# Sampled attention stream: the order of key gathers and value gathers on GpSimd

## Chip, cores, metric

The kernel runs on one core of a Trainium2 chip as a single launch. The metric is the device time of that launch in microseconds (us). The engines are named as in the profile: PE is TensorE (PEld its weight loads), DVE VectorE, ACT ScalarE, POOL GpSimd, SP SyncE (it only issues transfers).

## What is computed

One inference step of a one-layer decoder. A prompt of 2048 tokens and 8 sampled sequences of 8 new tokens each go through a shared input projection, then through FoX attention (softmax attention with a forgetting bias) beside an mLSTM, an output projection, layer norm, a squared-ReLU MLP and a second layer norm. The part that the change touches is the attention of the sampled tokens over a paged cache of 8192 old keys and values for each sequence:

```python
k_past = cache_k[l][page_table].reshape(DB, past, FOX_HEADS, FOX_HEAD_DIM)
v_past = cache_v[l][page_table].reshape(DB, past, FOX_HEADS, FOX_HEAD_DIM)
...
s_past = jnp.einsum('bqhd,bkhd->bhqk', q, k_past).astype(jnp.float32) * scale
s_past = s_past + Ln[..., :, None] + R[:, :, None, :]
...
p = jax.nn.softmax(jnp.concatenate([s_past, s_new], axis=-1), axis=-1).astype(v_new.dtype)
o = jnp.einsum('bhqk,bkhd->bqhd', p[..., :P], v_past) + jnp.einsum('bhqk,bkhd->bqhd', p[..., P:], v_new)
```

Keys and values together are 512 pieces of 512 KB (256 of each, 128 partitions by 1024 float32), fetched page by page through the page table.

## The kernel before

The prompt's work is done in stages: the input projection with the mLSTM (stage B and M in the code's letters, up to about 920 us), the prompt's FoX attention (about 920 to 1340 us), the output projection (about 1340 to 1600 us) and the MLP (about 1600 us to the end, matmuls into `ph` and `py`). The sampled attention is a Python generator, `sample_attention`, whose 295 steps are traced in between that work: `tick` counts the prompt's matmul time, and each time a pace is exceeded one more `step(n)` of the generator is traced. No step is traced during the prompt's FoX attention.

Within a step the names are:

- `k_gather(n)` (L1665) issues one indirect transfer from POOL that lands one key piece in the ring `kT`. Four pieces make a group. `k_turn(n)` (L1670) transposes a landed piece in place on DVE. `qk_step(g)` multiplies the queries with group g on PE into `sQ` (L1697) and thereby frees the ring's places.
- `v_gather()` (L1774) issues two indirect transfers from POOL (L1785), the two halves of one value step, into a pair of buffers. `vt` is always there; a second pair, `vx` in the output projection and `xr` in the MLP, is lent by the prompt's work. `pv_step` multiplies the softmax weights with these halves on PE into `sO` (L1809), the second half first, and thereby frees the pair.
- For the first 19 groups (`GA`), the ring holds one group: pieces 4g to 4g+3 are fetched in two steps after `qk_step(g-1)`. From group 19 on, the ring holds three pairs of pieces, and step n fetches piece n into the place of piece n-6. One `qk_step(k-1)` then frees the places of four pieces: 4k+2 and 4k+3, which complete group k, and 4k+4 and 4k+5, the first half of group k+1.

All instructions are laid out by a scheduler that replays a timeline while it orders each engine's queue; a program's order on PE, DVE, ACT and POOL is what it finds, within the dependencies and the priorities of the traced order. `tc.issue_after(ins)` is a hint to it alone: instructions traced within the block stand behind `ins` on that engine's queue, and no semaphore is added. Each engine then works through its queue in order, so on POOL a gather that waits for a place holds up everything behind it, the layer norms of the prompt's work (L173, L177) and the mLSTM's products (L765, L767) included.

Of the kernel before, what the change touches and what calls it, by code (L numbers as in the profile page):

```python
# [1530 lines left out]
def sample_attention(tc, I, O, ps_, pps, cst, ident, sqk, dnl, dR, dmix, dqb, vx, kx, pe, ring_a):  # L1531

    nc = tc.nc
    V, A, G, T, SY = nc.vector, nc.scalar, nc.gpsimd, nc.tensor, nc.sync
# [32 lines left out]
    cv = I["cache_v"][0].rearrange("g (t f) h d -> (g t) (f h d)", f=2)  # L1567
# [48 lines left out]
    for g in range(2):  # L1616
        p = pps.tile([32, 8, 64], F32, name="sT", tag="sX", bufs=1)
# [22 lines left out]
    def piece(n):  # L1640

        return kx["ring"][:, n // 2 % 2, n % 2] if n < NA else kx["ring"][:, (n - NA) // 2 % 3, n % 2]

    def q_load(b):
        qt = ps_.tile([128, 2, 16, 8], F32, name="qt", bufs=2)
        for n in range(2):
            SY.dma_start(qt[:, n].rearrange("p d t -> p (d t)"), dap(dqb, (n * NB + b) * 4096, [[0, 4], [128, 32], [1, 128]]))
        bn = ps_.tile([128, 2, 8], F32, name="bn", bufs=2)
        for hg in range(2):
            SY.dma_start(bn[:, hg], dap(dnl, hg * 4 * TOT + S + b * 8, [[TOT, 4], [0, 32], [1, 8]]))  # L1650
        state[b] = dict(qt=qt, bn=bn, U=[])
# [11 lines left out]
        mx = ps_.tile([128, 2, 17], F32, name="mxs", bufs=2)  # L1663
        z.update(qb=qb, kr=z["qt"][:, 1], Sn=Sn, mx=mx)

    def k_gather(n):
        b, j = divmod(n, 32)
        G.indirect_dma_start(out=piece(n), out_offset=None, in_=ck, in_offset=IO(ap=idxK[:, b, j // 2, j % 2:j % 2 + 1], axis=0))  # L1668

    def k_turn(n):  # L1670

        for i in range(2):
            x = piece(n)[:, i * 512:(i + 1) * 512]
            V.transpose(x, x)  # L1674
# [8 lines left out]
    def qk_step(g):  # L1683

        b, kt = divmod(g * 2, 16)
        z = state[b]
        rb = z["rb"]
        a0 = piece(4 * g)
        d = 1 if g < GA else (2 * (g - GA) + 1) % 3 - 2 * (g - GA) % 3
        pq = pps.tile([128, 2, 256], F32, name="sQ", tag="sX", bufs=1)  # L1690
        for hg in range(2):
            for db in range(2):
                for h4 in range(4):
                    hd = (hg * 4 + h4) * 2 + db
                    kv = bass.AP(tensor=a0.tensor, offset=a0.offset + hd * 32,
                                 ap=[list(a0.ap[0]), [d * 2048, 2], [512, 4], [1, 32]])
                    r = T.matmul(pq[h4 * 32:h4 * 32 + 32, hg].rearrange("p (k f c) -> p k f c", k=2, f=4), z["qb"][:, hd], kv,  # L1697
                                 start=(db == 0), stop=(db == 1), skip_group_check=True)
        if kt % 4 == 0:
            z["U"].append(ps_.tile([128, 2, 4, 4, 32], F32, name="S", tag="S", bufs=4))  # L1700
        for k in range(2):
            c = slice(k * 128, k * 128 + 128)
            for hg in range(2):
                V.tensor_tensor_reduce(out=z["U"][kt // 4][:, hg, :, kt % 4 + k], in0=pq[:, hg, c].rearrange("p (b t) -> p b t", t=32),
                                       in1=rb[:, hg, c].rearrange("p (b t) -> p b t", t=32), scale=1.0, scalar=NEG,
                                       op0=OP.add, op1=OP.max, accum_out=z["mx"][:, hg, kt + k:kt + k + 1])
        return r

    def softmax(b):
        z = state[b]  # L1710
        pq = pps.tile([128, 2, 256], F32, name="sQ", tag="sX", bufs=1)
        for hg in range(2):
            for db in range(2):
                for h4 in range(4):
                    hd = (hg * 4 + h4) * 2 + db
                    T.matmul(pq[h4 * 32:h4 * 32 + 32, hg, 0:8], z["qb"][:, hd], z["kr"][:, hd],
                             start=(db == 0), stop=(db == 1), skip_group_check=True)
        for hg in range(2):
            V.tensor_tensor_reduce(out=z["Sn"][:, hg], in0=pq[:, hg, 0:8], in1=z["bn"][:, hg], scale=1.0, scalar=NEG,
                                   op0=OP.add, op1=OP.max, accum_out=z["mx"][:, hg, 16:17])  # L1720

        V.tensor_reduce(mt[:, 0:2], z["mx"], axis=AX.X, op=OP.max)
        m2 = ps_.tile([128, 32], F32, name="m2", bufs=2)
        V.transpose(m2, mt)
        m3 = ps_.tile([128, 8], F32, name="m3", bufs=2)
        V.tensor_reduce(m3, m2.rearrange("p (g q) -> p q g", q=8), axis=AX.X, op=OP.max, negate=True)
        V.tensor_copy(m2.rearrange("p (g q) -> p g q", q=8), m3[:, None, :].to_broadcast([128, 4, 8]))
        m4 = ps_.tile([128, 32], F32, name="m4", bufs=2)
        V.transpose(m4, m2)
        rp = z["rp"] = ps_.tile([128, 2, 5], F32, name="rp", bufs=2)  # L1730
        for u in range(4):
            for hg in range(2):
                x = z["U"][u][:, hg].rearrange("p b k t -> p (b k t)")
                A.activation(x, x, AF.Exp, bias=m4[:, hg:hg + 1], accum_out=rp[:, hg, u:u + 1])
        for hg in range(2):
            A.activation(z["Sn"][:, hg], z["Sn"][:, hg], AF.Exp, bias=m4[:, hg:hg + 1], accum_out=rp[:, hg, 4:5])
# [34 lines left out]
    def v_new(b):  # L1771
        vn = state[b]["vn"] = ps_.tile([8, 512], F32, name="vns", bufs=1)
        SY.dma_start(vn, O["v_sample"][0, b].rearrange("t h d -> t (h d)"))

    def v_gather():

        p = vx["next"]
        b, kt = divmod(p, 16)
        vx["next"] += 1
        place = 0 if 0 not in vx["live"] else 1  # L1780
        vx["live"].append(place)
        vx["of"][p] = []
        for f in range(2):
            vt = (ps_.tile([128, 1024], F32, name="vt", bufs=2) if place == 0 else vx["more"]()).rearrange("p (f c) -> p f c", f=2)
            G.indirect_dma_start(out=vt.rearrange("p f c -> p (f c)"), out_offset=None, in_=cv,  # L1785
                                 in_offset=IO(ap=idxV[:, b, (kt % 4) * 4 + kt // 4, f:f + 1], axis=0))
            vx["of"][p].append(vt)

    def v_room():
        return kx["free"] and vx["next"] < 128 and len(vx["live"]) < (2 if vx["more"] else 1) and (0 not in vx["live"] or vx["more"])  # L1790
# [43 lines left out]
    def at(n, first, of):  # L1834

        i, r = divmod(n - first, of)
        return i if r == 0 and i >= 0 else None
# [4 lines left out]
    def step(n):  # L1842
        after = None
        if n == 0:
            q_load(0)
        g, r = divmod(n - 2, 4)
        if 0 <= g < GA and r >= 2:
            k_turn(4 * g + 2 * r - 4)
            k_turn(4 * g + 2 * r - 3)
        if NA + 2 < n < 258:  # L1850
            if n == NA + 3:
                k_turn(NA)
            k_turn(n - 2)
        g = at(n, 6, 4)
        if g is not None and g < 64:
            after = qk_step(g)
        b = at(n, 35, 32)
        if b is not None and b < 8:
            softmax(b)
        due = (n - 38) // 2 if n > NA + 2 else (n - 39) // 2  # L1860
        lead = 2
        while done[0] < 128 and done[0] - (lead == 1 and done[0] % 2) <= due and got.get(done[0], n) <= n - lead:
            after = pv_step(done[0] // 16, done[0] % 16, after)
            done[0] += 1
            lead = 1
        b = at(n, 70, 32)
        if b is not None:
            pv_end(b)
        b = at(n, 39, 32)
        if b is not None and b < 8:  # L1870
            softmax_new(b)
            v_new(b)
        b = at(n, 41, 32)
        if b is not None and b < 8:
            softmax_sum(b)
        u = at(n, 37, 8)
        if u is not None and u < 32:
            for hg in range(2):
                weights(u // 4, u % 4, hg)
        b = at(n, 30, 32)  # L1880
        if b is not None and b < 7:
            q_load(b + 1)
        b = at(n, 3, 32)
        if b is not None and b < 8:
            q_begin(b)
        g = at(n, 4, 4)
        if g is not None and g < 64:
            r_load(g)
        if n >= 35 and (n % 2 == 1 or not vx["live"]):
            while v_room():  # L1890
                got[vx["next"]] = n
                v_gather()
        g, r = divmod(n - 2, 4)
        if 0 <= g < GA and r < 2:
            k_gather(4 * g + 2 * r)
            k_gather(4 * g + 2 * r + 1)
        if NA + 6 <= n < 256:
            k_gather(n)

    done, got = [0], {}  # L1900
    for n in range(295):
# [32 lines left out]
```

## Time and profile before

| | us |
|---|---|
| median of 3 runs | 3321.62 (3318.09 to 3328.27) |
| the profiled execution's own time | 3319.55 |
| its span, first to last instruction | 3317.4 |
| PE busy | 3208.5 |
| DVE busy | 2120.5 |
| ACT busy | 1356.3 |
| POOL busy | 927.7 |
| mean granted TensorE clock | 0.991 |

The busy times are unions over an engine's instructions; PE's includes matmuls that overlap in its pipeline. The idle time of PE in the span is 3317.4 - 3208.5 = 108.9 us. The queries used below are the list of waits (who was idle, until what came, the total, the number and the longest), the timeline (start, duration, engine, line, what is written and read, how many merged, and in brackets the idle time before it and what ended it) and the windows (busy time of each engine in a stretch, then the granted clock, the busy share of the 16 DMA engines and the rate).

### The profile page before, as it was taken

To read this page: it belongs to the slowest core of one execution; us is meant where nothing else is said; L and a number is where in the kernel's file an instruction comes from. 1 tells how busy PE (TensorE), PEld (TensorE's weight loads), DVE (VectorE), ACT (ScalarE), POOL (GpSimd) and SP (SyncE) were. 2 spreads that over 40 slices of the span, in tenths; PEclk is the share of its full clock that TensorE was granted. 3 is DMA by queue.
4 is the path that set the end of the run, shared out by engine and by line. 5 is a ranking of instruction groups with operands and counts; after the bars stand their busy time and mean duration, and the time that the engine had idled before them with its cause. 6 is when DMAs were issued, how large, how long until landed. Compare 5 with 4: busy or idle time off the path is not lost. (4 is left out here: it accounts for less than half of the span.)

```text
span 3317.4 us, 57296 instructions
## 1 busy us (share of the span) xinstructions
PE 3208.5 (97%) x21420; PEld 2635.4 (79%) x21420; DVE 2120.5 (64%) x5161; ACT 1356.3 (41%) x2670; POOL 927.7 (28%) x1060
## 2 busy tenths in 40 slices
PE   9999999899999999999999999999999999999998
PEld 8998797787877777677777777777767777889997
DVE  6857567567577777555666667666666545655555
ACT  4444245344367777312333333232333333433332
POOL 0111122322344444465332225324252210100001
PEclk9999999999999999999999999999999999999999
DMA  5665765877642223677776778768587654532222
GB/s 173 167 191 179 217 212 183 262 253 236 221 123 84 77 83 115 245 277 259 269 265 226 267 239 316 246 231 289 200 281 263 205 182 141 162 127 87 87 82 67
DMA packets 427293, 646.22 MB, mean 195 GB/s; under 512 B 83148, under 2 KB 320016, under 8 KB 426120
## 3 DMA queue, kind: packets, MB, share of 16 engines
q1 hardware_dynamic: 350184, 363.09, 36.3%
q0 software_dynamic: 74304, 270.57, 22.0%
q10 hardware_dynamic: 2528, 8.91, 0.7%
q8 instruction: 169, 2.77, 0.3%
q14 instruction: 108, 0.88, 0.1%
HBM read 589.63 MB, written 52.83 MB: 194 GB/s over the span
## 5 line engine op out<-in xcount | busy, mean ns | idle before, releaser
L1489 DVE TENSOR_TENSOR y<-y,py 128x512 f32<-128x512 f32 x475 | 319.6, 680 | 277.2 <-PE py L159 262.2
L149 ACT ACTIVATE wh<-wr 128x1024 fp32r<-128x1024 f32 x268 | 278.4, 1056 | 472.9 <-PE py L159 256.8
L1674 DVE STREAM_TRANSPOSE kT<-kT 128x512 f32<-128x512 f32 x512 | 329.7, 685 | 219.0 <-DMA kT<-cache_k,idxK 218.5
L1668 POOL DMA_INDIRECT kT<-cache_k,idxK x256 | 264.9, 1035 | 715.4 <-PE sQ L1697 588.9
L157 PE MATMUL ph<-x1h,wh 128*128 128x512 f32 (+1 forms) x1280 | 454.1, 355 | 3.8 <-ACT wh L149 2.8
L158 PE MATMUL ph<-x1l,wh 128*128 128x512 f32 (+1 forms) x1280 | 452.7, 354 | 1.2 <-DVE x1l L152 1.2
L159 PE MATMUL ph<-x1h,wl 128*128 128x512 f32 (+1 forms) x1280 | 450.6, 353 | 1.9 <-DVE wl L152 1.7
L157 PE MATMUL py<-wh,h 128*128 128x512 f32 x1024 | 401.4, 397 | 4.6 <-DVE y L1489 3.4
L158 PE MATMUL py<-wl,h 128*128 128x512 f32 x1024 | 401.9, 393 | 0.2 <-DVE wl L152 0.2
L159 PE MATMUL py<-wh,h 128*128 128x512 f32 x1024 | 402.0, 393 | 0.0
L152 DVE TENSOR_TENSOR wl<-wr,wh 128x1024 fp32r<-128x1024 f32 x268 | 334.1, 1254 | 83.6 <-PE ph L159 36.2
L157 PE MATMUL pm<-whi,xhT 128*128 128x256 f32 (+2 forms) x1040 | 302.7, 291 | 2.4 <-ACT acb L542 1.4
L158 PE MATMUL pm<-wlo,xhT 128*128 128x256 f32 (+2 forms) x1040 | 298.3, 287 | 0.0
L159 PE MATMUL pm<-whi,xlT 128*128 128x256 f32 (+2 forms) x1040 | 297.3, 286 | 0.0
L157 PEld LDWEIGHTS ph<-x1h,wh 128*128 128x128 f32 x1280 | 241.1, 188 | 39.1 <-ACT wh L149 3.0
L159 PEld LDWEIGHTS ph<-x1h,wl 128*128 128x128 f32 x1280 | 241.0, 188 | 37.3 <-DVE wl L152 3.5
L158 PEld LDWEIGHTS ph<-x1l,wh 128*128 128x128 f32 x1280 | 241.2, 188 | 35.6 <-issue 2.5
L1785 POOL DMA_INDIRECT vt<-cache_v,idxV x156 | 155.6, 997 | 323.8 <-PE sO L1809 267.2
L157 PEld LDWEIGHTS py<-wh,h 128*128 128x128 f32 x1024 | 192.6, 188 | 53.0 <-issue 9.0
L1451 ACT ACTIVATE hq<-ph 128x512 f32<-128x512 f32 (+1 forms) x160 | 82.6, 516 | 361.0 <-PE ph L159 299.5
L159 PEld LDWEIGHTS py<-wh,h 128*128 128x128 f32 x1024 | 192.7, 188 | 46.2 <-issue 6.2
L158 PEld LDWEIGHTS py<-wl,h 128*128 128x128 f32 x1024 | 192.8, 188 | 39.0 <-issue 2.1
(420 smaller groups left out, 6747.4 us busy)
## 6 DMA issues: line engine op xcount, KB each, us to landing
wr<-w SPq DMA_DIRECT2D x256, 512.0 KB
wra<-w_in SPq DMA_DIRECT2D x112, 512.0 KB
Rb<-dR SPq DMA_DIRECT2D x128, 128.0 KB
wr<-w_o SPq DMA_DIRECT2D x16, 512.0 KB
xr<-dmix SPq DMA_DIRECT2D x16, 512.0 KB
y<-x_prompt SPq DMA_DIRECT2D x16, 512.0 KB
dx<-y SPq DMA_DIRECT2D x16, 512.0 KB
xr<-dx SPq DMA_DIRECT2D x16, 512.0 KB
```

The source lines that it names most:

```text
L149: last["ACT"] = A.activation(dst, src, AF.Copy, scale=scale)
L152: r = (eng or V).tensor_tensor(dst, src, hi.bitcast(F32), op=OP.subtract)
L157: T.matmul(ps, wh, xh, start=first, stop=False)
L158: T.matmul(ps, wh, xl, start=False, stop=False)
L159: last["PE"] = T.matmul(ps, wl, xh, start=False, stop=stop)
L1451: A.activation(hq, ps, AF.Relu)
L1489: V.tensor_tensor(y, y, ps, op=OP.add)
L1668: G.indirect_dma_start(out=piece(n), out_offset=None, in_=ck, in_offset=IO(ap=idxK[:, b, j // 2, j % 2:j % 2 + 1], axis=0))
L1674: V.transpose(x, x)
L1785: G.indirect_dma_start(out=vt.rearrange("p f c -> p (f c)"), out_offset=None, in_=cv, in_offset=IO(ap=idxV[:, b, (kt % 4) * 4 + kt // 4, f ...
```

## The change

`k_gather` takes a flag `late`. With it, the gather is traced in a block that queues it on POOL behind the last value gather that was traced before it (`vx["last"]`). The flag is set for the second half of each four: for r == 1 in the first 19 groups, and for r >= 2 after that, which are pieces 4k+4 and 4k+5. The instructions, their number, their buffers and their semaphores' partners stay the same.

```diff
-    def k_gather(n):
+    def k_gather(n, late=False):
         b, j = divmod(n, 32)
+        if late and "last" in vx:
+            with tc.issue_after(vx["last"].ins):
+                return k_gather(n)
         G.indirect_dma_start(out=piece(n), out_offset=None, in_=ck, in_offset=IO(ap=idxK[:, b, j // 2, j % 2:j % 2 + 1], axis=0))
...
-            G.indirect_dma_start(out=vt.rearrange("p f c -> p (f c)"), out_offset=None, in_=cv,
+            vx["last"] = G.indirect_dma_start(out=vt.rearrange("p f c -> p (f c)"), out_offset=None, in_=cv,
                                  in_offset=IO(ap=idxV[:, b, (kt % 4) * 4 + kt // 4, f:f + 1], axis=0))
...
         if 0 <= g < GA and r < 2:
-            k_gather(4 * g + 2 * r)
-            k_gather(4 * g + 2 * r + 1)
+            k_gather(4 * g + 2 * r, r == 1)
+            k_gather(4 * g + 2 * r + 1, r == 1)
         if NA + 6 <= n < 256:
-            k_gather(n)
+            k_gather(n, r >= 2)
```

The scheduler lays out the other engines anew as well. Three places show what moved. Lines behind the inserted three carry numbers larger by 3 in the changed kernel (L1668 is L1671, L1785 is L1788, L1697 is L1700, L1809 is L1812).

POOL in the mLSTM's stage, around the product `qi` (L767) that the profile before has at 587 us. Before:

```order
L1668 DMA kT<-cache_k,idxK 128x1024 x2
L1785 DMA vt<-cache_v,idxV 128x1024
L1668 DMA kT<-cache_k,idxK 128x1024 x2
L1785 DMA vt<-cache_v,idxV 128x1024
L767 TENSOR_TENSOR qi<-qi,qk 128x512
L765 AFFINE_SELECT qi<-qi 128x512
L1785 DMA vt<-cache_v,idxV 128x1024 x2
L1668 DMA kT<-cache_k,idxK 128x1024 x4
L1785 DMA vt<-cache_v,idxV 128x1024 x2
```

And changed:

```order
L1671 DMA kT<-cache_k,idxK 128x1024 x2
L1788 DMA vt<-cache_v,idxV 128x1024 x2
L1671 DMA kT<-cache_k,idxK 128x1024 x2
L1788 DMA vt<-cache_v,idxV 128x1024 x2
L767 TENSOR_TENSOR qi<-qi,qk 128x512
L765 AFFINE_SELECT qi<-qi 128x512
L1671 DMA kT<-cache_k,idxK 128x1024 x2
L1788 DMA vt<-cache_v,idxV 128x1024 x2
L1671 DMA kT<-cache_k,idxK 128x1024 x2
L1788 DMA vt<-cache_v,idxV 128x1024 x2
```

The value pair that stood behind `qi` now stands ahead of it, and the four key gathers are split in two and two around a value pair.

POOL in the MLP, at a place that the profile before has at 2029 to 2045 us, where the last layer-norm additions (`y`, L177) of one block of tokens meet a group of gathers. Before:

```order
L173 TENSOR_TENSOR ln<-ln,nhalf 128x1
L177 TENSOR_TENSOR y<-y,b_22506 128x1024 x2
L1668 DMA kT<-cache_k,idxK 128x1024 x4
L1785 DMA vt<-cache_v,idxV 128x1024 x2
L1785 DMA xr<-cache_v,idxV 128x1024 x2
L1668 DMA kT<-cache_k,idxK 128x1024 x4
```

And changed:

```order
L173 TENSOR_TENSOR ln<-ln,nhalf 128x1
L1671 DMA kT<-cache_k,idxK 128x1024 x2
L1788 DMA vt<-cache_v,idxV 128x1024 x2
L1788 DMA xr<-cache_v,idxV 128x1024 x2
L1671 DMA kT<-cache_k,idxK 128x1024 x2
L177 TENSOR_TENSOR y<-y,b_22506 128x1024
L1671 DMA kT<-cache_k,idxK 128x1024 x2
L1788 DMA vt<-cache_v,idxV 128x1024 x2
```

Two key gathers stand ahead of the values instead of four, two behind them, and the last addition moved behind the whole group.

PE in the MLP, at `qk_step(45)` and the value steps 74 (`vt`) and 75 (`xr`), which the profile before has at 2096 to 2107 us. Before:

```order
L158 MATMUL ph<-x1l,wh 128x512
L1697 MATMUL sQ<-kT,qb 32x256 x16
L1809 MATMUL sO<-vt,PTs 32x256 x8
L159 MATMUL ph<-x1h,wl 128x512
...
L158 MATMUL py<-wl,h 128x512
L1809 MATMUL sO<-xr,PTs 32x256 x8
```

And changed:

```order
L159 MATMUL py<-wh,h 128x512
L1700 MATMUL sQ<-kT,qb 32x256 x16
L1812 MATMUL sO<-vt,PTs 32x256 x8
L1812 MATMUL sO<-xr,PTs 32x256 x8
L158 MATMUL ph<-x1l,wh 128x512
```

Before, 21 matmuls of the MLP stand between the two value steps; now none does. The distance from `qk_step(44)` to `qk_step(45)` is 46 MLP matmuls before and 49 now.

## The prediction

> **What bounds the kernel now.** I read the page first, then PE's waits, then the timeline at the longest of them.
>
> ```profile
> span 3317.4 us, 57296 instructions
> PE 3208.5 (97%) x21420; PEld 2635.4 (79%) x21420; DVE 2120.5 (64%) x5161; ACT 1356.3 (41%) x2670; POOL 927.7 (28%) x1060
> ```
>
> PE sets the end: it is busy for 3208.5 us of 3317.4, and the change neither adds nor removes a matmul. It can only act on the 108.9 us in which PE is idle, and on the clock. PE's waits that have to do with the stream (total, number, longest):
>
> ```profile
> PE sO L1809 <- DMA vt<-cache_v,idxV: 23.3, 11, 5.0
> ...
> PE py L157 <- DVE y L1489: 3.4, 3, 1.7
> ...
> PE sO L1809 <- DMA xr<-cache_v,idxV: 0.9, 3, 0.4
> ```
>
> Value gathers that land too late are the largest wait of PE: 24.2 us with `xr`. No wait of `sQ` on keys is on the list; keys are waited for by DVE. The ten waits that make up nearly all of it:
>
> ```profile
> 599.06 1.51 PE L1809 MATMUL sO<-vt,PTs 128*32 128x256 f32 x12 [4.96 <-DMA vt<-cache_v,idxV]
> 627.31 0.62 PE L1809 MATMUL sO<-vt,PTs 128*32 128x256 f32 x2 [3.06 <-DMA vt<-cache_v,idxV]
> 784.16 1.07 PE L1809 MATMUL sO<-vt,PTs 128*32 128x256 f32 x16 [2.31 <-DMA vt<-cache_v,idxV]
> 1718.62 0.65 PE L1809 MATMUL sO<-vt,PTs 128*32 128x256 f32 x4 [2.51 <-DMA vt<-cache_v,idxV]
> 1824.36 0.85 PE L1809 MATMUL sO<-vt,PTs 128*32 128x256 f32 x12 [1.30 <-DMA vt<-cache_v,idxV]
> 2055.93 1.19 PE L1809 MATMUL sO<-vt,PTs 128*32 128x256 f32 x10 [3.43 <-DMA vt<-cache_v,idxV]
> 2100.26 1.07 PE L1809 MATMUL sO<-vt,PTs 128*32 128x256 f32 x16 [1.88 <-DMA vt<-cache_v,idxV]
> 2257.51 1.06 PE L1809 MATMUL sO<-vt,PTs 128*32 128x256 f32 x15 [0.76 <-DMA vt<-cache_v,idxV]
> 2305.23 1.07 PE L1809 MATMUL sO<-vt,PTs 128*32 128x256 f32 x16 [1.59 <-DMA vt<-cache_v,idxV]
> 2538.91 0.85 PE L1809 MATMUL sO<-vt,PTs 128*32 128x256 f32 x12 [1.24 <-DMA vt<-cache_v,idxV]
> ```
>
> The first three are 10.3 us, the seven in the MLP 12.7 us. What a group of gathers does before such a wait, at 2084 us:
>
> ```profile
> 2084.43 0.94 POOL L1668 DMA_INDIRECT kT<-cache_k,idxK  x1 [17.22 <-PE sQ L1697]
> 2085.68 0.94 POOL L1668 DMA_INDIRECT kT<-cache_k,idxK  x1 [0.31 <-issue]
> 2089.05 1.30 DVE L1674 STREAM_TRANSPOSE kT<-kT 128x512 f32<-128x512 f32 x2 [1.34 <-DMA kT<-cache_k,idxK]
> 2089.42 0.94 POOL L1785 DMA_INDIRECT vt<-cache_v,idxV  x1 [0.30 <-issue]
> 2090.67 0.94 POOL L1785 DMA_INDIRECT vt<-cache_v,idxV  x1 [0.30 <-issue]
> 2095.89 0.39 PE L157 MATMUL ph<-x1h,wh 128*128 128x512 f32 x1
> 2096.12 0.39 PE L158 MATMUL ph<-x1l,wh 128*128 128x512 f32 x1
> 2096.44 1.93 PE L1697 MATMUL sQ<-kT,qb 128*32 128x256 f32 x32
> 2106.24 1.07 PE L1809 MATMUL sO<-xr,PTs 128*32 128x256 f32 x16
> ```
>
> POOL issues a gather every 1.25 us. The first key has landed at 2089.05, when DVE's wait ends; the second `vt`, the sixth transfer of the group, at 2100.26, when PE's does. So five transfers took 11.2 us, 2.24 us each: the transfers, not the issues, set the pace. The same pair of readings is the ground for all seven waits in the MLP.
>
> **The change, part by part.** *Issues.* As many gathers as before, each about 0.94 us on POOL; nothing is added. Only their order differs, and no wait is new on the chip.
>
> *Values in the MLP.* Two keys stand ahead of the values instead of four, so `vt` lands 2 x 2.24 = 4.5 us earlier, more than any of the seven waits (0.76 to 3.43). If PE's order stayed, all 12.7 us would go. It does not stay: `xr`'s step, which stood 21 matmuls behind `vt`'s at this place, now stands right behind it. The second `xr` is now the sixth transfer; it lands when `vt` used to, and is needed only one value step later (1.0 us, the 1.07 us row at 2100.26). What is left of a wait is thus itself less 1.0 us, less what PE now has to do more between the two `qk_step`s. A matmul of the MLP counts 0.23 us (2095.89 to 2096.12). At 2100 us there are three more: 1.88 - 1.0 - 0.7 = 0.2. In the changed order the distance is the same for the waits at 1718 and 1824 (1.5 and 0.3 left), four matmuls more at 2305 (1.59 - 1.0 - 0.9, nothing), 25 more at 2257 and more at 2538 (nothing). The wait of 3.43 us has a cause of its own:
>
> ```profile
> 2026.59 1.93 PE L1697 MATMUL sQ<-kT,qb 128*32 128x256 f32 x32
> 2029.04 3.31 POOL L177 TENSOR_TENSOR y<-y,b 128x1024 f32<-128x1024 f32 x1 [2.30 <-DVE y L176]
> 2032.51 1.25 POOL L1668 DMA_INDIRECT kT<-cache_k,idxK  x1 [0.16 <-issue]
> ```
>
> The group stood behind a layer-norm addition and began at 2032.51, though `qk_step(42)` had freed its places by about 2028.5 (2026.59 + 1.93). In the changed order the addition stands behind the group: 4.0 us earlier. PE has 19 matmuls fewer ahead of this step (89 to 70 between the two `qk_step`s, 4.4 us), so `vt` has 4.0 + 4.5 - 4.4 = 4.1 us more than before, and needs 3.43. `xr`, nine matmuls behind it now, has 4.0 - 4.4 + 1.0 + 2.1 = 2.7 us: 0.7 is left. Sum of what is left in the MLP: 1.5 + 0.3 + 0.7 + 0.2 = 2.7 of 12.7. Gain **10.0**; bounds 12.7 (all) and, if `xr` inherits every wait in full, 0.
>
> The Trainium skill's page DMA: Bandwidth & Descriptors (Anatomy of one DMA — SWDGE (gpsimd) path) speaks for less: it fits a GpSimd transfer as 2.0 us plus its bytes over 436 GB/s, so that 512 KB more in a queue cost an estimated 1.2 us. By it two keys fewer bring `vt` forward by no more than their two issues, 2.5 us, and the wait at 2055 would keep some 1.3 us instead of 0.7; the sum would be 0.6 us smaller. The rows say 2.24 us a transfer, with the weights' transfers on the same engines.
>
> *Values in the mLSTM's stage.* The first wait has its cause on POOL:
>
> ```profile
> 584.88 0.39 PE L1809 MATMUL sO<-vt,PTs 128*32 128x256 f32 x3
> 587.04 1.30 POOL L767 TENSOR_TENSOR qi<-qi,qk 128x512 f32<-128x512 f32 x1 [15.32 <-ACT den L769]
> 590.54 0.94 POOL L1785 DMA_INDIRECT vt<-cache_v,idxV  x1 [0.30 <-issue]
> 616.73 1.90 POOL L1785 DMA_INDIRECT vt<-cache_v,idxV  x1 [5.35 <-PE sO L1809]
> ```
>
> The pair was free at 585.3 and was issued from 589.27 (one issue ahead of 590.54), behind `qi`, which waited for ACT. Now it stands ahead of `qi`: 3.7 us earlier, 1.3 of 4.96 left. The gathers for 627 (616.73) waited for the pair itself, no key being ahead of them: 3.06 stays. At 784 the second `vt` is the sixth of its group, split as in the first list of POOL; two keys fewer ahead give 4.5 us against 2.31: nothing left. Gain 10.3 - 4.4 = **5.9**; bounds 10.3 and 0, since the other engines' order there is new too.
>
> *Clock.* Windows of 3.4 us at three waits (busy times, granted clock, DMA share, GB/s):
>
> ```profile
> 1718.40:1721.80 3.40, 3.18 (x19) 1.72 (x20) 1.26 (x9) 0.00 (x0) 2.60 (x3) 0.50 1.07 402
> 2056.30:2059.70 3.40, 3.40 (x21) 2.04 (x11) 0.00 (x0) 0.00 (x0) 2.53 (x3) 0.50 1.06 416
> 627.00:630.40 3.40, 3.09 (x30) 2.38 (x34) 0.66 (x4) 0.85 (x3) 0.00 (x0) 1.00 0.02 5
> ```
>
> After the waits of 2.51 and 3.43 us PE ran 3.4 us at half clock; after that of 3.06 it did not. Each dip costs half its length, 1.7 us. I count the first two as gone: **3.4**; bounds 0 and 5.1 (the dip at 599 too).
>
> The Trainium skill's page TensorE: Matmul & The Clock Gate (Part 1: The HAM clock gate) has the gate close after an idle window of about 3.4 us, free-running. By that rule the dip at 1718 is not owed to its wait of 2.51 us, and the sum would be 1.7 us smaller; the row that shows it right at the wait decides for me.
>
> *Late keys.* The second half of each four now lands behind two to four values: up to 4 x 2.24 = 9.0 us later. It is read by PE one group later, but `k_turn` on DVE, which is in order, comes two steps after the gather. In the MLP (1600 to 2800 us) DVE waits for keys already:
>
> ```profile
> L1674 DVE STREAM_TRANSPOSE kT<-kT 128x512 f32<-128x512 f32 x288 | 186.0, 687 | 115.2 <-DMA kT<-cache_k,idxK 114.9
> ```
>
> Behind a waiting transpose on DVE stand the additions that empty `py` (L1489), for which PE waits. 114.9 us of DVE's waits go with 3.4 us of PE's (`py` from L1489, above). If DVE's waits double, I charge as much again: **-3.4**; bounds 0, and the loss of the second rival.
>
> Sum: 10.0 + 5.9 + 3.4 - 3.4 = 15.9 us. Against the profiled execution's own 3319.55 us (2.1 below the median of the runs, 3321.62): 3303.7, say **3304 us**.
>
> **Rivals.** *First: the scheduler spends the gain.* It placed `xr` right behind `vt` because its own timeline has the transfers sooner than the chip; with the stream laid out anew, waits of `xr` and in the mLSTM's stage come back. For it: the PE order shows exactly that move. Against it: `xr` has 1.0 us of `vt`'s own step before it, and most waits in the MLP are under 2 us. If two thirds of the 24.2 us stay and one dip goes: 24.2 / 3 + 1.7 - 3.4 = 6.4 us, 3313 us.
>
> *Second, slower: late keys stop DVE.* A transpose that waits 9.0 us holds the additions of `py`. Its three banks take six matmuls each, 3 x 6 x 0.23 = 4.1 us, before PE stops, so each such wait costs 4.9 us. 288 transposes are 144 pieces, 36 groups in the MLP. The gains without the charge are 19.3 us: from four such groups on they are gone, and with eight, 3319.55 - 19.3 + 39 = 3339 us. For it: DVE already waits for keys in the same stage. Against it: the scheduler orders DVE by the same timeline and has only the transfers' real pace wrong, and the present 114.9 us reach PE as 3.4.
>
> *Third: all of it goes.* Every value wait and the three dips: 24.2 + 5.1 = 29.3, 3290 us. For it: 4.5 us exceed all waits but one. Against it: the wait at 627 that the order leaves alone.
>
> That the order would not change is excluded by the lists of POOL.
>
> **How the numbers follow.** Forecast 0.50, first rival 0.23, second 0.15, third 0.12. What this kernel's measurement can tell from no change is about 0.3%, 10 us: 3311.7 and 3331.6 around the median. Faster takes the forecast and the third rival, 0.62; no change the first, 0.23; slower the second, 0.15. The range runs from just above the third rival, 3291, over the first rival to the point where the second is a few groups deep, 3328. The forecast's own range is 3297 to 3311 (the MLP's part 7 to 12.7, the mLSTM's 3 to 10.3, with the clock).
>
> **What would show it.** Right: in the changed profile PE's waits on `vt` and `xr` together are some 7 us instead of 24.2, no wait at the places of 784, 2055 and 2257 us, the wait of the 627 place still there, the half-clock windows at 1718 and 2056 gone, and PE's busy time the same but for the clock. The pace of 2.24 us a transfer should hold. Wrong: waits on `xr` of over 2 us right behind `vt`'s steps (first rival); PE's wait for `y` (L1489) or `wl` (L152) of over 15 us with DVE's waits on `kT` in the MLP far above 114.9 us (second). New waits between other engines at places where the scheduler's layout changed by chance, which no row here shows, would also make it wrong.

## The result and the profile after

The changed kernel takes 3317.01 us in the median of 18 runs (3310.10 to 3329.70), the kernel before 3326.71 us in 18 (3314.26 to 3341.13). The ratio is 0.997, 95% interval 0.996 to 0.998: about 9.7 us faster, where 15.9 were forecast. The forecast time of 3304 us lies 13.0 us below the measured one; 7.2 of these come from its base, the profiled execution of 3319.55 us, which is that much below the median of the 18. The time lies in the stated range (3291 to 3328), but not in the forecast's own (3297 to 3311).

One profile is too few to see 0.3%. The profile after is of an execution of 3323.93 us, 7 above its median; that of before was of 3319.55, 7 below the median of the 18 runs. So the two first profiles say the change costs 5 us of span, and the medians say the opposite. Below, each kernel is therefore read from three profiles. The page of the changed kernel (span, then the busy time of each engine):

```profile
span 3322.2 us, 57307 instructions
PE 3208.5 (97%) x21420; PEld 2637.1 (79%) x21420; DVE 2121.7 (64%) x5161; ACT 1357.2 (41%) x2670; POOL 931.2 (28%) x1060
```

PE's busy time is that of before to the tenth. The list of PE's waits of the changed kernel (total, number, longest), as far as it concerns values and the MLP:

```profile
PE sO L1812 <- DMA vt<-cache_v,idxV: 10.2, 7, 2.2
PE ph L157 <- ACT wh L149: 7.3, 2, 5.0
PE sO L1812 <- DMA xr<-cache_v,idxV: 6.8, 5, 3.4
PE px L1284 <- DMA xr<-dx: 4.9, 2, 2.6
...
PE ph L159 <- DVE wl L152: 4.1, 3, 2.9
...
PE py L157 <- DVE y L1489: 3.1, 2, 2.2
```

And the rows of the same list of before that the prediction did not show:

```profile
PE ph L157 <- ACT wh L149: 2.8, 1, 2.8
...
PE ph L159 <- DVE wl L152: 1.7, 3, 0.8
...
PE px L1284 <- DMA xr<-dx: 0.8, 1, 0.8
```

Waits for `vt` and `xr` fall from 24.2 to 17.0 us (17.8 with one of 0.8 for `vx`). Three others, which were 5.3 us together, are 16.3: for the weights' high half (`wh`), for their low half (`wl`), and for the prompt's rows (`xr<-dx`, a tile of the MLP that lies in the same buffers as the lent value pair). Two places of the timeline of the changed kernel:

```profile
2088.09 1.07 PE L1812 MATMUL sO<-vt,PTs 128*32 128x256 f32 x16 [1.00 <-DMA vt<-cache_v,idxV]
...
2092.57 1.47 PE L1812 MATMUL sO<-xr,PTs 128*32 128x256 f32 x16 [3.41 <-DMA xr<-cache_v,idxV]
```

```profile
2507.66 1.06 ACT L149 ACTIVATE wh<-wr 128x1024 fp32r<-128x1024 f32 x1 [11.56 <-DMA wr<-w]
...
2508.77 0.79 PE L157 MATMUL ph<-x1h,wh 128*128 128x512 f32 x1 [5.03 <-ACT wh L149]
```

The first is the place for which the prediction worked out 0.2 us: `xr`, now right behind `vt`, waits 3.41. The second is new: a weight tile that lands 11.56 us after ACT was ready for it holds PE for 5.03. On VectorE, the transposes of the keys between 1600 and 2800 us wait longer (groups by line; count, busy, mean, then idle time ahead of them):

```profile
L1677 DVE STREAM_TRANSPOSE kT<-kT 128x512 f32<-128x512 f32 x290 | 188.3, 687 | 143.0 <-DMA kT<-cache_k,idxK 142.8
```

That is 142.8 us where it was 114.9.

For the rest I summed the trace's idle intervals of PE by what the next matmul writes: values (`sO` that waits for a gather), MLP's kind (`ph`, `py`, `px`, and the output projection's `pw`), and the rest. Beside them stand the time at half clock (granted clock 0.50), PE's busy time, and VectorE's idle time at key transposes. The span is idle plus busy, but for some 16 us that follow PE's last matmul. Gaps under 0.15 us have no releaser in the trace and are counted by their place, so the columns are good to some 0.2 us. Of the labels, "again" are runs of the two kernels as they are, and "held" are explained with the experiments.

| us | values | MLP's kind | rest | idle, sum | half clock | PE busy | DVE at keys | span |
|---|---|---|---|---|---|---|---|---|
| before | 24.2 | 28.7 | 39.7 | 92.7 | 65.5 | 3208.5 | 219 | 3317.4 |
| before_again | 25.1 | 30.5 | 37.6 | 93.2 | 91.2 | 3215.9 | 219 | 3325.4 |
| held_before | 25.8 | 33.0 | 35.8 | 94.5 | 75.1 | 3212.0 | 223 | 3322.8 |
| after | 17.8 | 38.6 | 40.7 | 97.0 | 77.4 | 3208.5 | 273 | 3322.2 |
| after_again | 11.0 | 40.5 | 41.3 | 92.8 | 67.0 | 3202.4 | 261 | 3311.9 |
| held_after | 14.1 | 39.2 | 37.4 | 90.7 | 80.7 | 3208.0 | 264 | 3315.4 |

The means of three: waits for values 25.0 before and 14.3 after, 10.7 less; MLP's kind 30.7 and 39.4, 8.7 more; the rest 2.1 more. PE's idle time is 93.5 us before and after. **The stall that the change removes comes back at other places, in these profiles all of it.** What is left as a gain in them, 5.4 us of span, is PE's busy time, 5.8 us less. That is of the size of its scatter between executions of one program (3208.5 to 3215.9), which goes with the clock: half clock while PE was busy is 57.3 us before and 49.0 after (means of three), and half of that difference is 4.2 us. Over all executions, though, the clock does not tell the two kernels apart: on the chip of the run after_third (below) the mean granted clock is 0.9858 for both, in 12 executions of the changed kernel and 27 of the kernel before, at mean times of 3361.2 and 3367.0 us. So the measured 0.3% is not the clock alone. What else it consists of can't be told from six profiles, in which the idle time of one kernel scatters by up to 6 us (90.7 to 97.0); that PE's waits in all fell by far less than the waits for values can.

The table leaves out a fourth profile of the changed kernel, that of after_third: values 7.2 us, MLP's kind 62.1, rest 46.2, DVE at keys 156, span 3361.2. It is of a chip on which both kernels take over 1% longer, and the kernel before was not profiled there.

### The profile page after: what moved, and what is told of

It is laid out like the page before. It is cut to its first block, busy times and chain, and to the rows that moved or that the text cites. A ratio compares the mean times of both kernels' runs of the same rounds, so it can differ in the third digit from the quotient of the medians.

```text
span 3322.2 us, 57307 instructions
## 1 busy us (share of the span) xinstructions
PE 3208.5 (97%) x21420; PEld 2637.1 (79%) x21420; DVE 2121.7 (64%) x5161; ACT 1357.2 (41%) x2670; POOL 931.2 (28%) x1060
## 3 DMA queue, kind: packets, MB, share of 16 engines
q8 instruction: 169, 2.77, 0.3%
## 5 line engine op out<-in xcount | busy, mean ns | idle before, releaser
L1489 DVE TENSOR_TENSOR y<-y,py 128x512 f32<-128x512 f32 x475 | 319.0, 679 | 245.0 <-PE py L159 230.4
L1671 POOL DMA_INDIRECT kT<-cache_k,idxK x256 | 267.3, 1044 | 715.1 <-PE sQ L1700 626.3
L152 DVE TENSOR_TENSOR wl<-wr,wh 128x1024 fp32r<-128x1024 f32 x268 | 333.4, 1249 | 106.1 <-PE ph L159 40.7
L1788 POOL DMA_INDIRECT vt<-cache_v,idxV x156 | 162.8, 1044 | 316.1 <-PE sO L1812 261.5
L157 PEld LDWEIGHTS pm<-whi,xhT 128*128 128x128 f32 (+1 forms) x1040 | 198.4, 191 | 10.4 <-issue 5.3
```

The lines of the kernel that those rows point to most:

```text
L152: r = (eng or V).tensor_tensor(dst, src, hi.bitcast(F32), op=OP.subtract)
L157: T.matmul(ps, wh, xh, start=first, stop=False)
L1489: V.tensor_tensor(y, y, ps, op=OP.add)
L1788: vx["last"] = G.indirect_dma_start(out=vt.rearrange("p f c -> p (f c)"), out_offset=None, in_=cv, in_offset=IO(ap=idxV[:, b, (kt % 4) * 4 ...
```

## The experiments

Each ratio is to the kernel before on the same chip. The chips differ: the kernel before has a median of 3324 to 3327 us in the first measurement and on three chips after it, 3368 and 3377 on two more. Ratios are compared, not times.

### The same two kernels again, and each ring alone

The first two are the kernels as they are. In the third only the first 19 groups have late keys, in the fourth only the groups after them:

```diff
         if NA + 6 <= n < 256:
-            k_gather(n, r >= 2)
+            k_gather(n)
```

```diff
         if 0 <= g < GA and r < 2:
-            k_gather(4 * g + 2 * r, r == 1)
-            k_gather(4 * g + 2 * r + 1, r == 1)
+            k_gather(4 * g + 2 * r)
+            k_gather(4 * g + 2 * r + 1)
```

> The kernel before, unchanged. Its first profile was taken from an execution of 3319.55 us, 7 us below the median of its 18 runs; the changed kernel's first profile from one of 3323.93 us, 7 us above its median. If one execution is a poor sample of the waits: ratio 1.000 within 0.1%, but PE's total of waits and its list differ from the first profile by 5 to 10 us, mostly in waits that end with a transfer. If the first profile is typical: PE's waits on vt and xr are again 23 to 25 us in all and PE's idle time again 92 to 94 us between matmuls.

> The changed kernel, unchanged. Ratio 0.997 again (0.996 to 0.998). If the waits on values that came back are the loss (first rival): waits on vt, xr and vx again about 17 to 18 us, of which 10 in the MLP. If the loss is instead in waits that have nothing to do with values (weights, xr<-dx, x1l: about 14 us more than before in the first profile) and these are the scatter of one execution: they differ from the first profile, and a profile of an execution near 3317 us has fewer of them.

> The late flag for the first 19 groups only. By the sum of the prediction this part is worth 5.9 us (0.2%): ratio 0.998. If the order of the first 19 groups is worth only what the first profiles show (10.3 to 6.6 us of value waits there): ratio 0.999.

> The late flag for groups 19 to 63 only. By the sum of the prediction: 10.0 us of waits and 3.4 us of clock less 3.4, ratio 0.997. If xr inherits the waits as the first rival has it: PE's value waits in the MLP fall from 13.6 to about 10 us only, ratio 0.999 or more.

Measured: before_again 1.0004 (0.9986 to 1.0021), after_again 0.9987 (0.9971 to 1.0002), first ring alone 0.9981 (0.9967 to 0.9995), second ring alone 1.001 (0.9992 to 1.0028). As laid out here, the first ring's late keys carry what gain there is; the second ring's, in the stages where most of the forecast lay, bring nothing. (Each of the two is a layout of its own as well, and the next runs show how much a layout alone can move.) With the second ring alone the value waits behind 1595 us fall (13.9 to 7.5), and the waits of the MLP's kind there rise by as much (17.0 to 24.7). In the first ring alone they hardly do (19.4). So in these two layouts the return of the stall goes with the second ring.

### How much a new layout moves by itself

`PACE_C` says after how much of the prompt's matmul time a step of the stream is traced, behind the prompt's attention. A change of 0.4 or 2% adds and removes no work, but the scheduler lays everything out anew. The values 4.9, 5.1 and 5.02 were run with and without the change:

```diff
-PACE_C = 5
+PACE_C = 4.9
```

> The kernel before with PACE_C 4.9 instead of 5: the stream's steps are traced 2% closer together from the output projection on, and the scheduler lays out that part anew; the order of keys and values stays that of before. If PE's waits before the MLP's matmuls (weights, x1, y) in the MLP are a matter of each layout: they differ from the 17 to 18 us of before by 5 us or more. If they belong to the order of the gathers: 15 to 19 us again, and value waits in the MLP near 14 us.

> The changed kernel with PACE_C 4.9. If the new waits before the MLP's matmuls belong to the change (late keys and values laid into the blocks' boundaries): 23 to 28 us again, against before_pace49's 15 to 19, and value waits in the MLP 5 to 10 us. If they belong to one layout: anything between 12 and 30, with no order between the two kernels.

> The kernel before with PACE_C 5.1. As before_pace49: by the theory of chance the waits before the MLP's matmuls leave 15 to 19 us, by the theory of the gathers' order they stay there.

> The changed kernel with PACE_C 5.1. By the change's own effect: 23 to 28 us before the MLP's matmuls, 5 to 10 us of value waits in the MLP, and about 0.2% less time than before_pace51. By chance: no fixed difference to before_pace51 in the waits before the MLP's matmuls; the time differs by the sum of both.

> The kernel before with PACE_C 5.02, a step of 0.4% in the pace that gives the MLP another layout. By the theory that a new layout alone moves the time by some tenths of a per cent either way: a ratio that differs from 1 by 0.2% or more. By the theory that only the gathers' order counts: 1.000 within 0.2%.

> The changed kernel with PACE_C 5.02. By the change's own effect (0.25%): about 0.9975 of before_pace502. By chance of the layout: anything between 0.993 and 1.006 of it, as at 4.9 (0.993) and 5.1 (1.006).

| pace | before | changed | changed to before |
|---|---|---|---|
| 4.9 | 1.0122 (1.0099 to 1.0145) | 1.0052 (1.0035 to 1.0068) | 0.993 |
| 5 | 1.0004 (0.9986 to 1.0021) | 0.9987 (0.9971 to 1.0002) | 0.998 |
| 5.02 | 0.9962 (0.9948 to 0.9976) | 0.9958 (0.9945 to 0.9972) | 1.000 |
| 5.1 | 1.0009 (0.9995 to 1.0024) | 1.0068 (1.0048 to 1.0089) | 1.006 |

The last column divides the two. The rows are of different chips: 4.9 and 5.1 of one on which the pair at pace 5 was not run, 5.02 of the one on which after_third gave 0.9983. The effect of the change runs from 0.7% faster to 0.6% slower, by the layout that it meets, and the layout alone moves the kernel before by 1.6% (0.9962 to 1.0122). In all four pairs the value waits fall (pace 4.9: 16.1 to 14.5 us; 5.02: 20.3 to 6.3; 5.1: 14.6 to 10.8), though a fall as small as that at 4.9 is within the scatter of single profiles (11.0 to 17.8 in the changed kernel). The waits of the MLP's kind behind 1595 us move either way: 60.2 to 43.7 at 4.9, 30.4 to 38.2 at 5.02, 31.5 to 49.7 at 5.1, and their signs are those of the times at 4.9 and 5.1. Pace 5.02 without the change is as fast as with it.

### Late keys away from the block ends

The new waits for `wh`, `wl` and the prompt's rows lie where one block of the MLP ends and the next begins. There no `xr` pair is lent, so that this edit leaves the keys early there:

```diff
         if NA + 6 <= n < 256:
-            k_gather(n, r >= 2)
+            k_gather(n, r >= 2 and vx["more"] is not None)
```

> The changed kernel, but with the late flag in the second ring only while the second pair of buffers is lent, that is, not around the ends of the MLP's blocks of tokens; up to the first such end its order on PE is the changed kernel's. If the late keys at the block ends make the three new waits there (xr<-dx twice 2.5 us, wl 2.9, wh 5 to 7): these fall from 12 to 17 us to under 5, value waits in the MLP stay at 5 to 10, and the time is some 8 us (0.25%) less than the changed kernel's. If they come from the layout in general: waits of that size appear again at the block ends, at the same or other matmuls, and the time stays within 0.1% of the changed kernel's.

> The changed kernel again, on the same chip as the others of this call: ratio between 0.996 and 1.000, the new waits at the block ends (xr<-dx twice, wl, wh) there a third time.

Measured: 1.0001 (0.9984 to 1.0017), and the changed kernel beside it 0.9983 (0.9967 to 0.9999). The wait for `wh` near 2540 us (6.83 in after_third) is gone, but `py` waits 4.72 us for `y` at 2075 instead, and the stream's matmuls behind 1595 us wait 13.6 us (10.0 beside it). A wait that is pushed away at one place returns at another as long as the scheduler lays everything out anew: this run could not tell whether late keys or layout make it.

### The order of the other engines held

The instructions bear the same names in both kernels, so an order can be recorded and forced. `lay_out` chains each engine's instructions to a list of names; the edges concern the order alone and add no semaphore:

```diff
+def lay_out(tc):
+    by = {i.name: i for i in tc.nc.cur_bb.bb.instructions}
...
+            if last is not None:
+                tc.add_manual_dep(by[x], last, mybir.DependencyInfo(mybir.DependencyClass.NoSync, mybir.DependencyReason.DATA), reason="laid")
+            last = x
...
         body(tc, I, O, "SBMOC")
+        lay_out(tc)
```

held_before and held_after have the lists of the kernel before and of the changed kernel. In the other two, TensorE, VectorE, ScalarE and SyncE keep every place, and only the late keys move on GpSimd: in held_before_late, 68 keys of the second ring (pieces 82 to 221) go behind the values that directly followed them; in held_after_early all 105 late keys of the changed kernel go back ahead of theirs. Moving the first ring's keys, or the last of the second, in the layout of before was not tried: the engines' orders would wait for each other in a circle.

> The kernel before with every engine's instructions chained to the order that they already have: nothing moves, it is the base for the next run. Both theories: the time of before, ratio 0.999 to 1.001; value waits of about 25 us in all, MLP-part waits before px, ph and py of about 17 us.

> The order of every engine of before, kept, but for GpSimd's: 68 late keys of the second ring (pieces 82 to 221, two in each group) stand behind the values that directly followed them; TensorE, VectorE, ScalarE and SyncE keep every place. Theory A (the new layout that the scheduler makes gives the gain back): value waits of the MLP stage fall from 14 to 5 us, the waits before px, ph and py stay at 17, the time falls by 6 to 10 us against held_before (ratio 0.997 to 0.998). Theory B (the late keys themselves come in the way of weights and streams at the block ends): the value waits fall as much, the waits before px, ph and py grow by 6 or more, and the time stays within 3 us of held_before. Theory C (values are not brought sooner by the queue's order alone, since the 16 DMA engines are full): the value waits stay above 10 us, and the time stays.

> The changed kernel's order on every engine, chained: the base for the next run, and the time of the changed kernel. All theories: 0.996 to 0.999 of before; value waits of 11 to 18 us in all, MLP-part waits before px, ph and py of 24 to 27 us.

> The changed kernel's order on TensorE, VectorE, ScalarE and SyncE, with GpSimd's late keys put back ahead of the values that they were queued behind (105 of them). Theory A: the value waits rise by 7 to 14 us in all, the waits before px, ph and py stay at 24 to 27, and it is 6 to 12 us slower than held_after, so slower than before as well (ratio to before about 1.000 to 1.002). Theory B: the value waits rise as much, but the waits before px, ph and py fall to about 17, and the time stays within 3 us of held_after. Theory C: neither moves.

| | time, us | ratio | values | MLP's kind | rest | half clock | DVE at keys |
|---|---|---|---|---|---|---|---|
| held_before | 3321.00 | 0.9989 (0.9975 to 1.0004) | 25.8 | 33.0 | 35.8 | 75.1 | 223 |
| held_before_late | 3423.62 | 1.0306 (1.0286 to 1.0325) | 14.8 | 79.3 | 72.7 | 150.6 | 344 |
| held_after | 3311.51 | 0.9964 (0.9950 to 0.9978) | 14.1 | 39.2 | 37.4 | 80.7 | 264 |
| held_after_early | 3352.25 | 1.0084 (1.0064 to 1.0104) | 49.1 | 35.5 | 29.8 | 106.4 | 165 |

Chaining itself costs nothing that shows: held_before has the time of before, and held_after that of the changed kernel. The sizes of the other two were not expected: 6 to 12 us were the most that a theory gave. In the layout of before, the late keys do to the values what was forecast: behind 1595 us their waits fall from 14.5 to 3.2 us. But the time rises by 103 us. The list of PE's waits of held_before_late:

```profile
PE py L157 <- DVE y L1489: 18.9, 9, 5.0
PE sT L1766 <- ACT S L1734: 15.4, 3, 11.9
PE sT L1766 <- ACT PTs L1768: 14.3, 4, 10.6
PE sO L1809 <- DMA vt<-cache_v,idxV: 14.2, 7, 5.2
PE ph L159 <- DVE wl L152: 12.8, 7, 3.5
```

VectorE's wait for keys, at the key transposes of the whole program, in held_before:

```profile
L1674 DVE STREAM_TRANSPOSE kT<-kT 128x512 f32<-128x512 f32 x512 | 329.8, 685 | 223.0 <-DMA kT<-cache_k,idxK 222.5
```

and in held_before_late:

```profile
L1674 DVE STREAM_TRANSPOSE kT<-kT 128x512 f32<-128x512 f32 x512 | 330.9, 686 | 344.1 <-DMA kT<-cache_k,idxK 343.3
```

Two places of its timeline show how the one leads to the other. The first, on POOL, DVE and PE:

```profile
2101.63 1.78 POOL L1668 DMA_INDIRECT kT<-cache_k,idxK  x1 [0.30 <-issue]
2103.71 0.95 POOL L1668 DMA_INDIRECT kT<-cache_k,idxK  x1 [0.30 <-issue]
...
2119.29 1.30 DVE L1674 STREAM_TRANSPOSE kT<-kT 128x512 f32<-128x512 f32 x2 [9.94 <-DMA kT<-cache_k,idxK]
2121.03 1.30 DVE L1674 STREAM_TRANSPOSE kT<-kT 128x512 f32<-128x512 f32 x2 [0.43 <-DMA kT<-cache_k,idxK]
2122.26 1.25 DVE L1487 SCALAR_TENSOR_TENSOR y<-y,py 128x512 f32<-128x512 f32 x2
...
2122.96 0.79 PE L157 MATMUL py<-wh,h 128*128 128x512 f32 x1 [6.04 <-DVE y L1487]
```

The two late keys are issued behind four values at 2101 to 2104 and land 17 us later. VectorE, in order, stands at their transposes for 9.94 us; behind these stands the addition that empties `py`, and PE waits 6.04 us for it. This is the second rival of the prediction, near its own price (9.0 us and 4.9 were worked out).

The second place is in the output projection, where that rival expected nothing:

```profile
1534.05 1.31 DVE L1674 STREAM_TRANSPOSE kT<-kT 128x512 f32<-128x512 f32 x2 [4.68 <-DMA kT<-cache_k,idxK]
...
1537.35 0.20 DVE L1729 STREAM_TRANSPOSE m<-m 128x32 f32<-128x32 f32 x1
1537.59 0.72 ACT L1734 ACTIVATE S<-S,m 128x512 f32<-128x512 f32 x1 [16.19 <-DVE m L1729]
1538.45 1.12 PE L1766 MATMUL sT<-ident,S 128*128 128x128 f32 x4 [11.86 <-ACT S L1734]
```

The row maxima `m` of the softmax also stand behind waiting transposes on VectorE, ScalarE waits for them, and PE waits 11.86 us for ScalarE. Waits of the rest between 1335 and 1595 us rise from 5.3 to 27.1 us.

In the layout of the changed kernel the same order is worth 40.7 us: with the keys put back, VectorE waits 99 us less for keys, the waits of the MLP's kind fall by 3.7 and the rest by 7.6 (6.2 of it before 920 us, in the mLSTM's stage), and the waits for values rise by 35.0. One place in the two, with the same matmuls in the same order. held_after:

```profile
1702.81 0.95 POOL L1785 DMA_INDIRECT vt<-cache_v,idxV  x1 [0.30 <-PE py L159]
...
1704.38 1.30 DVE L1674 STREAM_TRANSPOSE kT<-kT 128x512 f32<-128x512 f32 x2 [1.83 <-DMA kT<-cache_k,idxK]
...
1714.16 1.05 PE L1809 MATMUL sO<-vt,PTs 128*32 128x256 f32 x16
1715.88 1.07 PE L1809 MATMUL sO<-xr,PTs 128*32 128x256 f32 x16 [0.67 <-DMA xr<-cache_v,idxV]
```

and held_after_early:

```profile
1718.68 1.31 DVE L1674 STREAM_TRANSPOSE kT<-kT 128x512 f32<-128x512 f32 x2 [1.94 <-DMA kT<-cache_k,idxK]
1719.50 0.96 POOL L1785 DMA_INDIRECT vt<-cache_v,idxV  x1 [0.31 <-issue]
...
1730.13 1.07 PE L1809 MATMUL sO<-vt,PTs 128*32 128x256 f32 x16 [1.61 <-DMA vt<-cache_v,idxV]
1733.35 1.07 PE L1809 MATMUL sO<-xr,PTs 128*32 128x256 f32 x16 [2.14 <-DMA xr<-cache_v,idxV]
```

From the landing of the first key to the second value of `xr` are five transfers in the one, 1704.38 to 1715.88, and seven in the other, 1718.68 to 1733.35: 2.3 and 2.1 us each. The layout leaves room for five; with two more keys ahead, both value steps wait.

So each layout fits its own order of gathers, and neither order is better by itself. With the keys first, the layout of before waits 25.8 us for values and the changed one 49.1; with the second ring's keys late, the layout of before waits 344 us on VectorE, and the changed one, with all of them late, 264. In time: with the keys first, the changed layout is 31.3 us slower than that of before (3352.25 and 3321.00), and the late keys make up 40.7 in it. The 9.5 us between held_before and held_after are what remains of these two.

As to the new waits at the block ends, held_after:

```profile
PE ph L159 <- DVE wl L152: 6.9, 4, 2.9
PE ph L157 <- ACT wh L149: 5.1, 2, 3.2
...
PE px L1284 <- DMA xr<-dx: 4.5, 2, 2.4
```

and held_after_early:

```profile
PE ph L157 <- ACT wh L149: 9.3, 2, 6.0
PE px L1284 <- DMA xr<-dx: 5.8, 2, 3.6
...
PE ph L159 <- DVE wl L152: 1.9, 3, 0.8
```

The waits for `wh` and for the prompt's rows stay when the keys go back: they belong to the layout. Those for `wl`, which VectorE makes, fall by 5.0, but more than half of that seems only to change its place: at the block end near 2490 us held_after waits 1.91 for `wh` and 2.94 for `wl`; held_after_early waits for neither there, but 6.04 for `wh` some 30 matmuls of the MLP further on. What goes with the late keys is the wait near 2013 us, 2.86 to 0.49 (1.58 when only the second ring's go back, in the run held_after_early_2nd below).

### The two rings, held

The same as held_after_early, with 20 keys of the first ring put back, or 85 of the second.

> The changed kernel's order on TensorE, VectorE, ScalarE and SyncE, with the 20 late keys of the first ring alone (mLSTM stage) put back ahead of the values that they were queued behind. If the two rings' shares add up from the waits that held_after and held_after_early show: the value waits before 920 us rise from 6.8 to about 17 us, other waits of that stage fall by about 5, those behind 1595 us stay at 6.5, and the time stands 6 to 10 us above held_after, some 0.999 of before. If the rings act on each other, the MLP's waits move too.

> The same with the 85 late keys of the second ring alone put back (attention over the prompt's tail and MLP stages). If the shares add up: the value waits behind 1595 us rise from 6.5 to about 27 us and those of 1335 to 1595 us to about 5, VectorE stands about 90 us less at key turns, the waits before px, ph and py behind 1595 us move by less than 3, and the time stands 24 to 32 us above held_after, some 1.004 to 1.006 of before. If only the first ring's order is worth anything, as the run with the first ring alone suggested, the time is that of held_after.

Measured: 1.0005 (0.9995 to 1.0015) and 1.0038 (1.0024 to 1.0051). Above held_after's 0.9964 that is 0.0041 and 0.0074 of some 3325 us, 14 and 25 us, together 38, where both at once made 40.7. The value waits before 920 us are 16.4 with the first ring put back (6.8 in held_after), those behind 1595 us 25.1 with the second (6.5). The times add up, the waits less plainly. Of PE's idle time the first ring moves only 2.2 us (90.7 to 92.9): with its keys early the waits of the rest before 920 us fall from 24.5 to 15.1, about as much as the values rise. Its 14 us go with PE's busy time (6.2 us more) and the clock, whose mean is 0.9864 over these executions and 0.9894 over held_after's, while the kernel before has 0.9884 and 0.9883 on the two chips. In a kept layout the second ring's order is worth more than the first's; it is only when the scheduler may lay out the rest anew that nothing of it is left.

## Why the prediction was partly wrong

**The mechanism of the values held.** Two keys fewer ahead bring the values forward, and the transfers set the pace: 2.24 us each by the prediction, 2.1 to 2.3 in the held pair. The Trainium skill's page DMA: Bandwidth & Descriptors (Anatomy of one DMA, SWDGE (gpsimd) path), by whose fit 512 KB more cost an estimated 1.2 us, is not borne out here. The weights are fetched through the same 16 engines at the time; that they make the difference was not tested.

**MLP values, forecast 10.0 us.** The waits for values behind 1595 us fell from 14.2 to 7.2 (means of three), 7.0. The prediction said that with PE's order kept all 12.7 would go; held_before_late, with that order kept, shows 14.5 to 3.2. That `xr` inherits part of a wait was seen, but at too little: 0.2 us were left for the place where 3.41 are.

**mLSTM values, forecast 5.9 us.** From 9.7 to 6.3 in the means, 3.4. In the profile after, waits of 1.84 us at 774.56 and 2.08 at 808.49 stand where the one of 2.31 at 784 was to vanish. The order of the other engines is new there too, as the bound of 0 said.

**Clock, forecast 3.4 us.** The half-clock stretches at 1718 and 2056 are gone, but others came, one at the 3.41 us wait shown above. In all, half clock is 77.3 us before and 75.0 after, half of the difference is 1.1, and executions of one program differ by 26. Nor does a given wait keep its price: the one near 626 us (3.06 in the first profile of before, without half clock) is 3.37 in before_again and held_before, with 6.8 us at half clock in both, and one of 2.77 at 1722 us of held_before has none.

**Late keys, forecast -3.4 us: the step that failed.** It charged one path, PE's wait for the `py` additions (L1489) behind VectorE's waiting transposes in the MLP, with a doubling, and put every other wait of PE at nothing. That path did not grow: 2.5 us before and 2.6 after (means of three), with VectorE's waits for keys in the MLP up from 115.0 to 138.8, not doubled. PE's waits for other things than values grew all the same, by 10.8 us (8.7 of the MLP's kind, 2.1 others), as much as the values gave: `wh` from 3.1 to 7.8, the prompt's rows from 1.1 to 4.7, `wl` from 3.0 to 4.9, and the rest in the mLSTM's stage from 23.5 to 26.6. The held pair tells two sources apart. In the changed layout the late keys themselves cost 11.3 us of such waits (76.6 with them, 65.3 without), 6.2 of them in the mLSTM's stage, for which the prediction charged nothing; the waits for `wh` and the rows come from the layout that the scheduler made around them. With 10.8 in place of 3.4, 10.4 us of values instead of 15.9 and 1.1 of clock, the sum is 0.7 us. The median's 9.7 us are more than that, and where they lie stays open; so the forecast's terms do not explain that the kernel became faster, and its being right about that is in part luck.

**The rivals.** The first (the scheduler spends the gain, 3313 us) is the nearest in time and kind, though it let the gain be spent on values alone. The second (late keys stop VectorE) is a true mechanism, 103 us strong when the orders of before are held. The changed kernel escapes most of it, it seems because the scheduler gave the transposes later places: with the keys first, VectorE waits 223 us for them in the layout of before and 165 in the changed one. The third did not occur. What was named at the end, new waits by chance of the layout, is what weighed most: the same change moves the time by -0.7 to +0.6% as the pace is varied by 2%.

**Still open.** Why the weights of the block at 2507 us land 11.56 us late is only half shown: the 16 DMA engines are busy for 0.98 to 1.04 of the time in every stretch from 2480 to 2508 us, and eight gathers issued between 2481 and 2493 land up to 2507.47, just ahead of these weights. But the kernel before has eight gathers and engines as full at that time; there ScalarE waits 3.20 us for weights, and PE for none. The largest gain of any run, pace 5.02 (0.9962 without the change and 0.9958 with it), equals the changed kernel's best reading, held_after's 0.9964, and none of these is a version clearly faster than both kernels.

## What to carry to other kernels

Where a scheduler lays out all engines anew, price a reordering of one queue as two changes: the queue's own order in the old layout, and the new layout; and look whether what the later transfers feed stands on an in-order engine ahead of work that the critical engine needs. A removed stall is a gain only if the next engine's queue can absorb the delay, so forecast the idle time in all and not the one row that the edit is aimed at. Before trusting an effect under 1%, vary a parameter that should not matter: if that moves the time as much, hold the orders of the other engines and change one alone.

## What the runs showed of the hardware

Waiting costs more than its own length. In held_before_late PE's idle time is 72.2 us above held_before's, and its busy time 27.4 above as well (3239.4 to 3212.0); in held_after_early idle rises by 23.8 and busy by 12.2. So 0.4 to 0.5 us of busy time come on top of each us of waiting. The time at half clock rises by 75.5 and 25.7 us; counted only where PE was busy, by 49.6 (56.5 to 106.1) and 27.0 (53.8 to 80.8). Half of these, 24.8 and 13.5 us, is near the 27.4 and 12.2. The Trainium skill's page TensorE: Matmul & The Clock Gate (HAM oscillation) counts half of the throttled time as the penalty of waits on transfers; both pairs agree, if half clock in idle time is left out.

Executions of one program on one chip spread over 24 us (3312.32 to 3336.75 in 22 runs of the kernel before, beside the held ones), more than twice the effect measured, and chips differ by 1.6% for the same kernel (3324 to 3377 us).
